# A two-layer decoder trunk on one core: first mixer's indexer and memory products in plain fp32, others in three products, new order of first loads

## Chip, cores and metric

The kernel runs on one core of one Trainium2 chip. The metric is the device time of one launch in microseconds, the median over several runs. Below, PE is TensorE (matmuls), PEld its weight loads, DVE VectorE, ACT ScalarE, POOL GpSimd, SP the SyncE queue that issues the loads.

## The reference, cut to what matters

512 tokens of width 1024 pass two layers. Each layer is `x += Mix(RMSNorm(x))`, then `x += SwiGLU(RMSNorm(x))`; a last RMSNorm follows. Layer 0 mixes by an indexer: eight small heads score every earlier key, the 128 best keys of a query are kept, and 12 heads (4 key/value heads, rotary) attend to those.

```python
logits = einsum('bqhd,bsd->bqhs', qib, ki)                  # 8 indexer heads, one shared key
score = einsum('bqhs,bqh->bqs', relu(logits), wib)
score = where(key_pos <= t_pos, score, NEG)
_, idx = top_k(score, min(256, seq // 4))                   # 128 keys
# 12 query heads attend to k[idx], v[idx]: softmax(q k / 8) v
# 4 memory heads, in both layers:
kv = rms_norm(mem, g_mem) @ w_mem_kv                        # 256 memory tokens
mo = softmax(qm @ kv_keys / 8) @ kv_values
x = x + concatenate([mix, mo]) @ w_out
```

Layer 1 mixes by dilated windows and attends to the same 256 memory tokens with its own weights. Everything is float32.

## The kernel before

Activations are kept transposed: `xT` holds eight tiles (k = 0 to 7) of 128 features x 512 tokens. A projection gives 128 output features x 512 tokens in one PSUM bank, over eight steps k. Each step is made of three matmuls in the type fp32r (`proj_steps`, `projs`, lines 217 to 227 with 213 to 215): weights and activations are split into a high part, rounded on ScalarE, and a low part, the rest, subtracted on VectorE or POOL (`_split2`, lines 48 and 51). High x high, high x low and low x high are summed. Value projections have tokens on the partitions and 256 columns (`token_major`). Attention scores take two heads at once, on rows 0 to 63 and 64 to 127 of the array, each again in three products (`scores`, line 414). Products of probabilities with values, transposes by the identity, the row that spreads the norm factors (`row`, line 268) and two of layer 1's value products (line 1017) are plain fp32.

TensorE executes in the order of the program; the other engines' order is planned by the compiler. Weights come in 1 MB loads of two chunks through two buffers (`wf`), split chunks lie in three buffers each for high and low (`wh`, `wl`). PSUM has banks by tag: acc 2, S 3, T 2, O 1.

`run` issues the first loads: gains, then x tiles and the first two weight chunks in turn, with frequencies and positions after the fourth x tile. `layer0` then runs so:

1. `angles` makes sine and cosine of the positions and writes them to DRAM, from where `angle_table` reads them back spread over the partitions. `prep` scales x by the norm's gains, splits it and sums its squares.
2. Five chunks of `in0` belong to the indexer: chunk 0 (the key and the head weights) and chunk 1 step by step together, then 2, 3 and 4. `ssq_cols` and `row` make the norm factors; `rope` rotates each result and splits it. `memory_load` and `memory_squares` (squares and sums both on POOL) start on the memory.
3. Chunk 5 (first key pair) starts; the column sums of the memory follow on TensorE (`ssq_cols(mem_parts)`, line 256), and then `logits` (relu on ScalarE, weighted sums on VectorE, lines 756 to 762), woven with chunk 5 and the value products of `value_steps`.
4. `memory_split`, the second key pair, two chunks of memory queries (`plain`), keys and values of the memory (`memory_kv`), then `memory_attention` woven with four query chunks. `topk` runs beside it on VectorE: 16 rounds of MAX8 and MATCH_REPLACE (lines 695, 696) for three blocks of queries, and a closing step (line 700).
5. 18 score units of the 12 heads, `exp_scores` (line 595) with the selection as bias, transposes and value products; between them the last two query chunks, layer 1's memory keys and values (`memory_ahead`, which loads the memory again, splits it and keeps the results in DRAM) and the output projection.

Then come `ffn(0)`, `layer1` and `ffn(1)`, all in three products but for what was named.

## Time and profile before

| | |
|---|---|
| median of 3 runs | 1267.03 us (1263.38 to 1268.05) |
| profiled execution | 1261.48 us, span 1259.8 us |
| mean granted clock of TensorE | 0.978 |
| busy, share of the span: PE / DVE / ACT / POOL | 95% / 46% / 40% / 31% |
| chain that ended last: PE / DVE / DMA | 78% / 13% / 3% |

The profile is of one execution. A busy time is the time in which at least one instruction of the engine ran; matmuls overlap, so a matmul's own duration is longer than its share, and the distance between starts is the better measure. The granted clock is given as a share of 2.4 GHz; its lower level is 1.2 GHz.

### The profile page before, as it was taken

To read this page: it belongs to the slowest core of one execution; us is meant where nothing else is said; L and a number is where in the kernel's file an instruction comes from. 1 tells how busy PE (TensorE), PEld (TensorE's weight loads), DVE (VectorE), ACT (ScalarE), POOL (GpSimd) and SP (SyncE) were. 2 spreads that over 40 slices of the span, in tenths; PEclk is the share of its full clock that TensorE was granted. 3 is DMA by queue.
4 is the path that set the end of the run, shared out by engine and by line. 5 is a ranking of instruction groups with operands and counts; after the bars stand their busy time and mean duration, and the time that the engine had idled before them with its cause. 6 is when DMAs were issued, how large, how long until landed. Compare 5 with 4: busy or idle time off the path is not lost.

```text
span 1259.8 us, 14831 instructions
## 1 busy us (share of the span) xinstructions
PE 1191.5 (95%) x5804; PEld 963.8 (77%) x5804; DVE 585.3 (46%) x1058; ACT 499.7 (40%) x865; POOL 385.7 (31%) x240
## 2 busy tenths in 40 slices
PE   6688989999999999999998999999999999999997
PEld 5467767677888888888887778887788888888886
DVE  7789986548433333322224544449533333332112
ACT  5564566524332233223223666545223223322222
POOL 4637374336122221121222223224222222211222
PEclk9789998999999999999999999999899999999999
DMA  5402222111222222222323120121122222222221
GB/s 180 137 34 70 82 90 99 56 49 68 100 101 88 84 97 100 100 62 104 110 105 127 67 71 34 68 67 67 67 100 101 94 81 93 101 92 92 92 92 67
DMA packets 30211, 109.96 MB, mean 87 GB/s; under 512 B 2494, under 2 KB 12094, under 8 KB 21694
## 3 DMA queue, kind: packets, MB, share of 16 engines
q1 hardware_dynamic: 29598, 108.50, 24.4%
q8 instruction: 45, 0.74, 0.2%
q10 hardware_dynamic: 544, 0.52, 0.1%
q14 instruction: 24, 0.20, 0.1%
HBM read 105.74 MB, written 3.28 MB: 87 GB/s over the span
## 4 chain that ended last, share of the span: by engine, by line
PE 78%; DVE 13%; DMA 3%; ACT 2%; POOL 2%; issue 2%; SPq 0%; DVEq 0%; POOLq 0%; ACTq 0%
PE psS L227 5%; PE psS L226 5%; PE psS L225 5%; PE psT L226 3%; PE psT L227 3%; PE psT L225 3%; PE psacc L227 3%; PE psacc L226 3%; PE psacc L225 3%; PE psacc L200 3%; PE psS L200 3%; PE psS L202 3%; PE psS L201 3%; PE psS L414 3%; PE psacc L202 3%; PE psacc L201 3%
## 5 line engine op out<-in xcount | busy, mean ns | idle before, releaser
L51 POOL TENSOR_TENSOR wl<-wf,wh 128x1024 fp32r<-128x1024 f32 x96 | 233.7, 2436 | 636.3 <-ACT wh L48 594.0
L48 ACT CAST wh<-wf 128x1024 fp32r<-128x1024 f32 x176 | 181.2, 1031 | 512.8 <-issue 164.2
L51 DVE TENSOR_TENSOR wl<-wf,wh 128x1024 fp32r<-128x1024 f32 (+1 forms) x93 | 116.0, 1247 | 90.9 <-ACT wh L48 90.9
L225 PE MATMUL psS<-xh,wh 128*128 128x512 f32 x296 | 117.8, 398 | 7.5 <-ACT wh L48 7.5
L227 PE MATMUL psS<-xh,wl 128*128 128x512 f32 x296 | 118.4, 400 | 2.6 <-DVE wl L51 2.6
L226 PE MATMUL psS<-xl,wh 128*128 128x512 f32 x296 | 117.6, 397 | 2.8 <-DVE xl L310 2.8
L227 PE MATMUL psT<-xh,wl 128*128 128x512 f32 x200 | 80.1, 400 | 0.0
L226 PE MATMUL psT<-xl,wh 128*128 128x512 f32 x200 | 79.8, 399 | 0.0
L225 PE MATMUL psT<-xh,wh 128*128 128x512 f32 x200 | 79.5, 398 | 0.0
L227 PE MATMUL psacc<-xh,wl 128*128 128x512 f32 x192 | 76.6, 399 | 0.0
L226 PE MATMUL psacc<-xl,wh 128*128 128x512 f32 x192 | 76.2, 397 | 0.0
L225 PE MATMUL psacc<-xh,wh 128*128 128x512 f32 x192 | 75.9, 395 | 0.0
L225 PEld LDWEIGHTS psS<-xh,wh 128*128 128x128 f32 x296 | 56.6, 191 | 20.3 <-ACT wh L48 7.5
L226 PEld LDWEIGHTS psS<-xl,wh 128*128 128x128 f32 x296 | 56.6, 191 | 16.8 <-DVE xl L310 3.3
L227 PEld LDWEIGHTS psS<-xh,wl 128*128 128x128 f32 x296 | 56.5, 191 | 15.4 <-DVE wl L51 4.0
L294 POOL TENSOR_TENSOR ssq<-ssq,t 128x512 f32<-128x512 f32 (+1 forms) x34 | 50.9, 1496 | 54.9 <-ACT t L284 53.8
L213 PE MATMUL psacc<-xh,wh 128*128 128x512 f32 x144 | 62.7, 435 | 0.0
L652 DVE TENSOR_TENSOR raw<-psacc,R 128x512 f32<-128x512 f32 x22 | 15.2, 691 | 100.8 <-PE psacc L227 100.8
L215 PE MATMUL psacc<-xh,wl 128*128 128x512 f32 x144 | 58.0, 403 | 0.0
L214 PE MATMUL psacc<-xl,wh 128*128 128x512 f32 x144 | 57.8, 401 | 0.0
L627 DVE TENSOR_TENSOR xT<-xT,psacc 128x512 f32<-128x512 f32 x44 | 30.0, 684 | 38.8 <-PE psacc L202 38.6
L339 POOL TENSOR_TENSOR raw<-raw,table 128x512 f32<-128x512 f32 x21 | 27.9, 1329 | 58.4 <-ACT raw L336 39.8
(339 smaller groups left out, 2729.0 us busy)
## 6 DMA issues: line engine op xcount, KB each, us to landing
wf<-in_gu SPq DMA_DIRECT2D x44, 1024.0 KB
wf<-in_dn SPq DMA_DIRECT2D x16, 1024.0 KB
wf<-in_in SPq DMA_DIRECT2D x13, 1024.0 KB
wf<-in_dn SPq DMA_DIRECT2D x16, 384.0 KB
wf<-in_v SPq DMA_DIRECT2D x3, 1024.0 KB
xT<-in_x SPq DMA_DIRECT2D x8, 256.0 KB
wf<-in_mk SPq DMA_DIRECT2D x2, 1024.0 KB
wf<-in_mv SPq DMA_DIRECT2D x2, 1024.0 KB
```

The lines of the kernel that those rows point to most:

```text
L48: nc.scalar.copy(hi, src)
L51: lo_engine.tensor_tensor(out=lo, in0=src, in1=hi.bitcast(F32), op=ALU.subtract)
L200: mm(out, wh[k], xh[k], start=first and k == 0, stop=False)
L201: mm(out, wh[k], xl[k], start=False, stop=False)
L202: mm(out, wl[k], xh[k], start=False, stop=last and k == n - 1)
L213: mm(out, wh[:, s], xh[k], start=k == 0, stop=False)
L214: mm(out, wh[:, s], xl[k], start=False, stop=False)
L215: mm(out, wl[:, s], xh[k], start=False, stop=k == KT - 1)
L225: mm(out, wh[:, s], xh[k], start=k == 0, stop=False)
L226: mm(out, wh[:, s], xl[k], start=False, stop=False)
L227: mm(out, wl[:, s], xh[k], start=False, stop=k == KT - 1)
L294: engine.tensor_tensor(out=parts[part], in0=parts[part], in1=sq, op=ALU.add)
```

## The change

- Order of the first loads: chunk 0, then all of x, chunk 1, frequencies, positions. TensorE first issues 14 matmuls of 128 columns whose result isn't used; `angles` moves behind the first two products and the column sums.
- `scaled` scales x on VectorE and keeps it whole; ScalarE squares, VectorE sums. The five indexer chunks are plain fp32 on it (`fp32_steps`), from the loaded buffer. `halves` splits x only after them, for the remaining chunks, which stay in three products with the low parts of chunk 5 from VectorE and of chunks 6 to 14 from POOL.
- Rotated queries and keys of the indexer and of the 12 heads stay whole (no split after `rope`); logits and scores of the first mixer are one fp32 product each. All of `rope_steps` multiplies and adds on POOL. Relu of the logits is done in place in PSUM, and their banks alternate between the tags S and acc.
- The memory, for both layers, is scaled on ScalarE and multiplied in fp32 from the loaded buffers; its squares move to ScalarE, the sums stay on POOL and are used after six of the twelve logit units. The memory is not loaded a second time. Keys kept for layer 1 are whole and half as large, and layer 1's memory queries and scores are fp32 as well.

```diff
+    def plain_chunks(self, name, order):
+        src = self.io[name]
+        for a in range(0, len(order), 2):
+            m = min(2, len(order) - a)
+            w = self.load(src[order[a]:order[a] + m].rearrange("t p n -> p t n"), [m, KT * 128])
+            for j in range(m):
+                yield w[:, j]
+    def fp32_steps(self, out, w, x):
+        for k in range(KT):
+            self.nc.tensor.matmul(out, w[:, k * 128:(k + 1) * 128], x[k], start=k == 0, stop=k == KT - 1)
+            if k % 2:
+                yield 1
+    def fp32_tokens(self, out, w, ks, x, b):
+        n = out.shape[-1]
+        for k in ks:
+            self.nc.tensor.matmul(out, x[k][:, b], w[:, k * n:(k + 1) * n], start=k == 0, stop=k == KT - 1)
...
+    def scaled(self, gi):
+        nc = self.nc
+        xg = []
+        add, parts = self.squares()
+        for k in range(KT):
+            if k % 4 == 0:
+                big = self.big("xg", F32)
+            t = big[:, (k % 4) * S:(k % 4 + 1) * S]
+            nc.vector.tensor_scalar(t, self.xT[:, k], self.gains[:, gi, k:k + 1], None, op0=ALU.mult)
+            add(self.xT[:, k], 0, nc.vector)
+            xg.append(t)
+        return xg, parts
+    def halves(self, x):
+        xh, xl = [], []
+        for k in range(KT):
+            if k % 4 == 0:
+                bh, bl = self.big("xh"), self.big("xl")
+            b = slice((k % 4) * S, (k % 4 + 1) * S)
+            _split2(self.nc, bh[:, b], bl[:, b], x[k], self.nc.vector)
+            xh.append(bh[:, b])
+            xl.append(bl[:, b])
+        return xh, xl
...
         (mul or nc.gpsimd).tensor_tensor(out=sw, in0=sw, in1=sn, op=ALU.mult)
-        (add or nc.vector).tensor_tensor(out=raw, in0=raw, in1=sw, op=ALU.add)
+        last = hi if lo is None and twice is None else raw
+        (add or nc.vector).tensor_tensor(out=last, in0=raw, in1=sw, op=ALU.add)
         if twice is not None:
-            nc.vector.tensor_tensor(out=raw, in0=raw, in1=twice, op=ALU.mult)
+            nc.vector.tensor_tensor(out=hi, in0=raw, in1=twice, op=ALU.mult)
+        if lo is None:
+            return hi
...
+        if units[0][2] is None:
+            for out, q, _, k, _, rows, qs, ks in units:
+                mm(out, q[rows, qs], k[rows, ks], start=True, stop=True)
+            return
...
-            add(m, 0, self.nc.gpsimd, self.nc.gpsimd)
+            add(m, 0, self.nc.gpsimd)
...
+    def memory_scaled(self, l, mem):
+        g = self.big("mg", F32)
         for k in range(KT):
...
+            self.nc.scalar.activation(g[:, k * MEM:(k + 1) * MEM], mem[k], AF.Copy,
+                                      scale=self.gains[:, 1 if l == 0 else 4, k:k + 1])
+        return [g[:, k * MEM:(k + 1) * MEM] for k in range(KT)]
+    def memory_kv(self, l, x):
+        for w in self.plain_chunks(f"mk{l}", [0, 1]):
             p = self.psum("acc")
+            for n, _ in enumerate(self.fp32_steps(p[:, :MEM], w, x)):
...
+            yield self.plain(p, self.mem_row, 1.0, "km", n=MEM)
+        w = self.load(self.io[f"mv{l}"], [KT * 256])
         for i in range(2):
...
+            self.fp32_tokens(p, w, range(4), x, b)
             yield None
+            self.fp32_tokens(p, w, range(4, KT), x, b)
...
     def layer0(self):
         nc, mm = self.nc, self.nc.tensor.matmul
-        self.angles()
-        xh, xl, parts = self.prep(0, early=4, squares=(1, 3))
-        first = [self.wsplit(self.first[j], nc.vector) for j in range(2)]
-        pk, pq = self.psum("S"), self.psum("S")
-        self.projs([(pk, first[0]), (pq, first[1])], xh, xl)
-        ws = itertools.chain(self.chunks("in0", [2, 3]), self.chunks("in0", [4, 5]),
-                             self.chunks("in0", list(range(6, 15)), lo=("gpsimd", "gpsimd")))
+        idle = self.psum("T")
+        for _ in range(14):
+            mm(idle[:, :128], self.ones, self.ones, start=True, stop=True)
+        x, parts = self.scaled(0)
+        ws = itertools.chain(self.first, self.plain_chunks("in0", [2, 3, 4]))
...
+        pk, pq = product("S"), product("S")
         cols = self.ssq_cols(parts)
+        self.angles()
...
-                ps = [self.psum("S") for _ in range(2)]
+                tag = ("S", "acc")[(j + i) % 2]
+                ps = [self.psum(tag) for _ in range(2)]
...
-                    t = self.tmp(("t", "o")[s])
+                    t = ps[s]
...
-            dst.append(self.rope(p, cs, sn, *out, add=nc.gpsimd, split=nc.gpsimd, mul=mul))
+            dst.append(self.rope(p, cs, sn, out, None, add=nc.gpsimd, mul=nc.gpsimd))
...
         index_q(3, p3)
-        steps = itertools.chain(rope_steps(K, kb[:, 0], kb[:, 1], tag="O"), value_steps())
-        next(steps)
+        xh, xl = self.halves(x)
+        ws = itertools.chain(self.chunks("in0", [5], lo=("vector",)), self.chunks("in0", list(range(6, 15)), lo=("gpsimd", "gpsimd")))
+        steps = itertools.chain(rope_steps(K, kb[:, 0], tag="O"), value_steps())
+        mem_parts = self.memory_squares(mem)
+        every = itertools.chain.from_iterable(logits(j) for j in range(4))
+        for _ in itertools.islice(steps, 4):
+            pass
+        _weave(itertools.islice(steps, 3), itertools.islice(every, 6), nb=2)
         self.mem_cols = self.ssq_cols(mem_parts, n=2, keep=True)
-        every = itertools.chain.from_iterable(logits(j) for j in range(4))
-        _weave(itertools.islice(steps, 12), every, nb=1)
+        _weave(itertools.islice(steps, 3), every, nb=2)
...
-        fill = itertools.chain(queries(2), self.memory_ahead())
+        fill = itertools.chain(queries(2), self.memory_ahead(mem))
...
+        nc.sync.dma_start(self.first[0], self.io["in0"][0])
         for k in range(KT):
             nc.sync.dma_start(self.xT[:, k], self.io["x"][k * 128:(k + 1) * 128, :])
-            if k < 2:
-                nc.sync.dma_start(self.first[k], self.io["in0"][k])
-            if k == 3:
-                nc.sync.dma_start(self.freq, self.io["freq"])
...
+        nc.sync.dma_start(self.first[1], self.io["in0"][1])
+        nc.sync.dma_start(self.freq, self.io["freq"])
```

## Rows read from the trace of the kernel before

**Rows 1.** Table by stretch: from:to, length, busy time (instructions) by engine, PEclk, DMA share.

```profile
0.00:100.00 100.00, 72.99 (x344) 56.08 (x345) 78.86 (x116) 57.86 (x102) 51.45 (x40) 0.90 0.36 121
100.00:170.00 70.00, 63.20 (x350) 50.04 (x348) 69.50 (x179) 37.84 (x78) 41.64 (x29) 0.95 0.19 68
170.00:290.00 120.00, 111.12 (x678) 82.46 (x677) 69.65 (x179) 61.29 (x162) 53.24 (x37) 0.97 0.21 69
...
320.00:677.00 357.00, 357.00 (x1561) 292.81 (x1560) 113.06 (x142) 105.36 (x129) 79.97 (x36) 1.00 0.26 95
```

**Rows 2.** TensorE's waits, 0 to 300 us: sum, times, longest.

```profile
PE psacc L256 <- POOL ssq L294: 9.1, 1, 9.1
PE psS L414 <- DVE nx L595: 8.2, 7, 3.7
...
PE psS L414 <- ACT t L756: 5.5, 3, 3.9
```

**Rows 3.** The chain that ended last, 25 to 105 us: start, duration, what.

```profile
31.96 11.39 DMA mem<-in_mem
...
59.45 1.03 PE psacc L256 x4
```

**Rows 4.** Order of time, VectorE, in the selection: start, duration, what.

```profile
104.66 1.47 DVE L695 MAX8 m<-score 128x8 f32<-128x512 f32 x3
...
107.63 1.47 DVE L695 MAX8 m<-score 128x8 f32<-128x512 f32 x3
...
168.84 4.22 DVE L700 TENSOR_SCALAR score<-score 128x512 f32<-128x512 f32 x3
```

**Rows 5.** Order of time, TensorE: memory scores, then the first mixer's scores.

```profile
131.33 0.39 PE L414 MATMUL psS<-km,qmh 64*128 64x256 f32 x2
...
172.16 0.33 PE L414 MATMUL psS<-k,qh 64*128 64x128 f32 x2
...
182.00 0.50 PE L414 MATMUL psS<-k,qh 64*128 64x512 f32 x2
...
182.90 0.50 PE L213 MATMUL psacc<-xh,wh 128*128 128x512 f32 x1
```

**Rows 6.** Table by stretch, TensorE alone: length, busy (matmuls), PEclk, DMA.

```profile
26.58:32.10 5.52, 5.52 (x26) 1.00 0.23 66
113.82:119.40 5.58, 5.58 (x49) 1.00 0.54 188
7.46:18.65 11.19, 8.58 (x18) 1.00 0.90 333
```

**Rows 7.** Order of time, TensorE: plain fp32 products of 512 and 256 columns.

```profile
319.43 1.02 PE L268 MATMUL psacc<-raw,ones 128*128 128x512 f32 x2
...
320.52 0.39 PE L226 MATMUL psS<-xl,wh 128*128 128x512 f32 x1
...
773.06 2.13 PE L1017 MATMUL psacc<-wf,xT 128*128 128x256 f32 x8
```

**Rows 8.** DMA in 0 to 60 us, 40 slices of 1.5 us.

```profile
GB/s 0 109 249 352 373 392 360 396 408 284 374 262 0 0 0 0 0 0 44 86 80 89 145 258 225 215 244 312 199 47 55 27 8 213 415 63 49 102 56 52
```

**Rows 9.** Order of time, VectorE: first use of the sine table, and layer 1's memory split.

```profile
42.93 0.69 DVE L339 TENSOR_TENSOR raw<-raw,table 128x512 f32<-128x512 f32 x1 [4.02 <-DMA table<-saved]
...
188.67 2.06 DVE L486 SCALAR_TENSOR_TENSOR ml<-wf,gains,mh 128x256 fp32r<-128x256 f32 x5
```

**Rows 10.** Order of time, SP and ScalarE: a weight load's issue and its first use.

```profile
113.92 0.34 SPq L176 DMA_DIRECT2D wf<-in_mv  x1
...
118.76 1.99 ACT L48 CAST wh<-wf 128x1024 fp32r<-128x1024 f32 x2 [1.84 <-DMA wf<-in_mv]
```

**Rows 11.** VectorE's groups, 101.6 to 172 us: line, operation, shapes, busy, mean ns.

```profile
L51 DVE TENSOR_TENSOR wl<-wf,wh 128x1024 fp32r<-128x1024 f32 x2 | 4.5, 2262 | 0.0
...
L51 DVE TENSOR_TENSOR km<-t,km 128x256 fp32r<-128x256 f32 x2 | 1.9, 975 | 0.0
```

More of the change, by code (lines that the diff above doesn't have):

```diff
@@ L490, in memory_kv @@
-    def memory_kv(self, l, m):
-        mh, ml = m
-        xh = [mh[:, k * MEM:(k + 1) * MEM] for k in range(KT)]
-        xl = [ml[:, k * MEM:(k + 1) * MEM] for k in range(KT)]
-        for w in self.chunks(f"mk{l}", [0, 1]):
+            self.nc.scalar.activation(g[:, k * MEM:(k + 1) * MEM], mem[k], AF.Copy,
[3 more added lines that the diff above has]
+        for w in self.plain_chunks(f"mk{l}", [0, 1]):
@@ L514, in memory_ahead @@
+            t = self.slot("vm", F32)[:, :256]
+            self.values(p, self.mem_cols[:, i:i + 1], t)
+            yield t
+    def memory_ahead(self, mem):
         nc = self.nc
-        mem = self.load(self.io["mem"].rearrange("(k p) n -> p k n", p=128), [KT, MEM])
-        m = self.memory_split(1, [mem[:, k] for k in range(KT)])
-        self.kept = self.dram.tile([4, 128, 512], F32, name="kept")
+        x = self.memory_scaled(1, mem)
+        self.kept = self.dram.tile([4, 128, 256], F32, name="kept")
@@ L518, in memory_ahead @@
         n = 0
-        for r in self.memory_kv(1, m):
-            if r:
-                n_cols = 512 if n < 2 else 256
-                nc.sync.dma_start(self.kept[n][:, :n_cols], r[1].bitcast(F32)[:, :n_cols])
+        for r in self.memory_kv(1, x):
+            if r is not None:
+                nc.sync.dma_start(self.kept[n], r)
                 n += 1
@@ L526, in memory_back @@
     def memory_back(self):
-        ts = []
-        for n in range(4):
-            ts.append(self.slot("kept", F32R if n < 2 else F32))
-            n_cols = 512 if n < 2 else 256
-            self.nc.sync.dma_start(ts[n].bitcast(F32)[:, :n_cols], self.kept[n][:, :n_cols])
-        self.mem_kv = [(t[:, :MEM], t[:, MEM:]) for t in ts[:2]], ts[2:]
+        ts = [self.slot("kept", F32)[:, :256] for _ in range(4)]
+        for n, t in enumerate(ts):
+            self.nc.sync.dma_start(t, self.kept[n])
+        self.mem_kv = ts[:2], ts[2:]
     def memory_attention(self, qm, early):
@@ L764, in logits, with rope_steps @@
                 yield 1
-        kb = self.big("k").rearrange("p (c n) -> p c n", c=4)
+        kv = self.big("kv", F32)
+        kb = kv[:, :1024].rearrange("p (c n) -> p c n", c=2)
+        V = kv[:, 1024:].rearrange("p (i n) -> p i n", i=NT)
         K, Q, qm = [], [], []
-        def index_steps(j):
-            p = self.psum("T")
-            yield from self.proj_steps(p, next(ws), xh, xl)
-            index_q(j, p)
-        def rope_steps(dst, *out, tag="acc", mul=None):
+        def rope_steps(dst, out, tag="acc"):
             p = self.psum(tag)
             yield from self.proj_steps(p, next(ws), xh, xl)
-            dst.append(self.rope(p, cs, sn, *out, add=nc.gpsimd, split=nc.gpsimd, mul=mul))
-        V = self.big("v", F32).rearrange("p (i n) -> p i n", i=8)
+            dst.append(self.rope(p, cs, sn, out, None, add=nc.gpsimd, mul=nc.gpsimd))
         def value_steps():
@@ L808, in layer0 @@
             qm.append(self.plain(p, R, 0.125, "qm", engine=nc.gpsimd))
-        mem = [r[0] for r in self.memory_kv(0, mem) if r]
-        self.mem_kv = mem[:2], mem[2:]
+        kept = [r for r in self.memory_kv(0, xm) if r is not None]
+        self.mem_kv = kept[:2], kept[2:]
         self.masks()
@@ L816, in queries @@
             for c in range(n):
-                yield from rope_steps(Q, self.slot("qh"), self.slot("ql"))
+                yield from rope_steps(Q, self.slot("q", F32))
         _weave(queries(4), mema, nb=1, na=1)
```

78 lines of the change are left out of this document (21 added, 57 removed).

## Prediction

> **What bounds the kernel now.** I read the stretch table first [rows 1]. From 320 to 677 us (the first FFN) TensorE is busy for all of 357 us, and the change doesn't touch that stage or the second FFN. So whatever moves must move in the first mixer, which ends some 20 us before that stretch, and in layer 1's memory attention. In 0 to 100 us TensorE is busy for 73 us, at a mean granted clock of 0.90, so a part ran at the lower level of 1.2 GHz. In 100 to 170 us VectorE is busy for 69.5 of 70: this is the top-k selection. From 170 to 290 us TensorE is the fuller engine, 111 of 120.
>
> Then the waits of TensorE up to 300 us [rows 2]. The longest, 9.1 us, is for POOL's sums of squares of the memory. The chain of waits puts its end at 59.45 us; the load it hangs on was in at 31.96 + 11.39 = 43.35 us, and POOL's squares and sums filled the 16 us between [rows 3]. TensorE executes in program order, so the logits, which need nothing of the memory, stand behind it. 5.5 us of waits are the logits' own (PSUM banks held until ScalarE has read them), 8.2 us those for the biased scores after the selection.
>
> The selection needs the last logits. One round of 16 takes 107.63 - 104.66 = 2.97 us, 47.5 us in all [rows 4]. Its first round starts one such step ahead of the row shown, at 101.7 us, and the closing step at 168.84, 67 us later: 19.6 us of other VectorE work are woven in. The first scores of the mixer proper issue at 172.16 us [rows 5]. So the path is: index products, memory stall, logits, selection, scores; behind that it is TensorE.
>
> **The price of fp32.** A chunk in three products, 8 steps of 3 matmuls with 512 columns, took 5.5 us, 0.69 a step; two chunks with 256 columns took 5.58 us, 0.35 a step [rows 6]. One fp32 product shows as two records. For 512 columns: the product that spreads R starts at 319.43, and the second matmul after it at 320.52; less the 0.23 us of the one between, that is 0.86 us. For 256 columns: eight records in 2.13 us, the last lasting some 0.40, give 0.247 each, 0.49 a product [rows 7]. The Trainium skill ("FP8 and Floating Point Precision", TensorE Precision Notes) says that true FP32 makes four passes through the array, which speaks against the change; by it a step would cost 4/3 of 0.69, an estimate of 0.92 us, and the five index chunks 1.6 us more than in the sum below. The row gives 0.86, so the sum goes by rows: 0.88 a step, with 0.86 and 0.98 (two 256-column products of 0.49) as bounds.
>
> **Part by part, up to the scores.**
> Loads and start. The first weight chunk is issued first, then the eight tiles of x, then chunk 1, frequencies, positions. The DMA slices of 1.5 us [rows 8] add up to 0.54 MB at 4.5 us, 2.2 at 9 and 2.75 at 10.5. So chunk 0 and x (2.6 MB) are in at about 10 us, chunk 1 at 11.5. No split stands before a product any more, only one scaling on VectorE. Before, the first 18 matmuls took 11.2 us, 8.6 of them busy [rows 6], with waits between them and at the lower clock. The 14 idle products run from 1 to about 6.5 us, so the clock should be up when x is there. From 6.2 us: five chunks x 8 steps x 0.88 = 35.2, plus 1 us for the column sums and 0.9 for R: the last index product ends near 43.3 us.
> Angles. Their issue moves behind all of x, so positions land with the last loads, at about 12 us. VectorE's queue ahead of them is shorter by two weight splits. Then the round trip through DRAM, for which VectorE waited until 42.93 us [rows 9]. I take it 4 us earlier. The ropes need about 10 us of VectorE and run beside the last index products and the key chunk.
> The splits of x become extra passes, eight each on ScalarE and VectorE. A VectorE operation of 512 columns takes 0.69 us [rows 9], so 5.5 us, which lie between 24 and 40 us, where VectorE waits for the tables. Without that cover they come on the path.
> Key chunk: 5.5 us, to 49. Then the value weights: their buffer is free only when the last fp32 product is done (43.3). A 1 MB load took 118.76 - 113.92 = 4.84 us from issue to use [rows 10], cast and low part 2.2: 50.4 us, a stall of 1.5.
> Logits. Six half value products of 1.4 us, twelve logit units, the column sums of the memory. A unit of 512 columns took 182.90 - 182.00 = 0.90 us with the changes of tile form [rows 5]; in fp32, with the two heads of a pair overlapping in the array as now, 0.86 and about 0.1 for the change of form. So nothing is added: 12 x 0.71 = 8.5 us for the three widths. The sum is 50.4 + 8.4 + 8.5 + 1 = 68 us. Five banks in place of three hold the logits. The memory sums now come after six units, with the squares on ScalarE: POOL keeps half of its 16 us, from about 41 us on, so I put the 9.1 us wait at zero. VectorE's 24 accumulations, at no more than 0.7 us each, run beside it. With 3 us of latency behind the last unit and 4 us of small stalls the selection starts at about 75 us, not 101.7.
> Selection. 47.5 us, 4 us of closing steps, and of the 19.6 us woven in 11 stay: two weight splits (4.5) and the low parts of the memory keys (1.9) are gone [rows 11], and three rope multiplies of 0.69 go to POOL. So VectorE is done at about 138 us.
> TensorE in that time: two half value products 2.8, second key chunk 5.5, two memory-query chunks 11, memory keys and values 32 products x 0.49 = 15.7 (were 11.2), a row 0.5, and the four query chunks with the memory attention woven in, 131.33 to 172.16 before [rows 5], 40.8 us; of these I take off 2 for waits on VectorE. 74.3 us from 70 us on: 145. TensorE has become the later of the two. Against 172.2: **27 us earlier**.
> POOL gains rope multiplies and loses low parts, one for one, and at 41.6 of 70 us [rows 1] it is no bound.
>
> **After the scores.** Of the 8.2 us of waits for biased scores [rows 2] most stood behind layer 1's memory split on VectorE (five of its operations from 188.67 us [rows 9]). With the split gone I take 6 us back, and 2.5 us of low clock after it. Layer 1's keys and values cost 32 x (0.49 - 0.35) = 4.5 us more. The scores come out even, as above. Net **-4 us**. In layer 1 the kept memory is smaller and two query splits go; the memory scores cost the same: 0 to -2, taken as 0.
>
> Sum: 27 + 4 = 31 us. The profiled execution has 1261.5 us (span 1259.8, 1.7 around it), 5.5 under the median of the three runs. 1261.5 - 31 = 1230.5; on the scale of the median **1236 us**.
>
> **Bounds.** No row shows fp32 products on 64 rows, so their overlap is bounded from both sides: as full as in the three-product form, or none. In columns per pair of heads the logits have 4608, the scores 7680, the memory scores 2 x 2048: 16,384, or 32 times 512 at 0.86 = 27.5 us more if pairs run one after the other. I take the overlap; the nearest row is the same code in the same tile form. On the other side: no stalls at all (-7), all of the 8.2 us back (-2), 0.86 a step (-1), layer 1 (-2): 12 us better.
>
> **Rivals.**
> Pairs in sequence (0.10). The 27.5 us come onto TensorE, which is the bound from 145 us on. The gain shrinks to 3 or 4 us: 1263. Against it: six matmuls of 512 columns on 64 rows fit into 0.90 us now, which only overlap allows. The Trainium skill ("TensorEngine Tiling (Array Packing)", Key Properties) says that different tiles load and multiply in parallel. By that rule this rival wouldn't occur; no row here shows it for fp32.
> The start isn't shortened (0.15). The index ropes, not the products, set the first logits: if the DRAM round trip of the tables still ends at 42.9 us, VectorE takes the x splits (5.5 us) ahead of the ropes and POOL's sums come late, the logits gain only half of the 27 us. Then 13 + 4: 1250.
> Held weight buffers (0.10), the slow side. An fp32 product reads the loaded buffer itself and frees it at its last step; there are two buffers. The split form frees it some 3 us after landing, far ahead. Eight hand-overs change that way (two index loads, the value weights, two query loads, two of layer 1's memory, the first output chunk). Each one exposed costs 4.84 us of load, and 3.5 of cast and POOL split where the next user is split: 8.3 us. I counted 1.5 us for the one I found exposed. From four exposed (33 us) the gain is gone; with five, 41 against 31, it is slower: 1277.
> The forecast as summed has 0.65.
>
> **How the numbers follow.** The forecast's own range is 1224 to 1248 (12 better; 12 worse if half the start's gain is lost in stalls). To leave out no more than 2 in 10 the range takes in the start rival and the pairs in sequence: 1222 to 1263. A measurement of this kernel can tell about 0.5%, 6.3 us. Faster: forecast 0.65, start 0.15 and a little of the pairs: 0.82. Same: the rest of the pairs and a share of the buffers: 0.10. Slower: 0.08.
>
> **What would show it.** Right: the first MAX8 near 75 us, the first scores near 145, the FFN's first products some 30 us earlier; no TensorE wait above 3 us for the memory's sums; fp32 records of 0.43 us at 512 columns; VectorE nearly full in the selection. The pairs are in sequence if the logit records of both heads lie end to end. The start is wrong if the first logit issues later than 57 us. Buffers are exposed if TensorE waits above 3 us for wf or wh more than twice. The prediction is wrong altogether if the first scores issue after 165 us.

## The result, and the profile after

The changed kernel takes **1257.28 us** (median of 20 runs, 1247.48 to 1262.89) beside 1263.5 us for the kernel before (20 runs, 1260.28 to 1273.14): a ratio of 0.993, 95% interval 0.991 to 0.995. Forecast were 1236 us with a range of 1222 to 1263: the direction and the range held, the size did not, 31 us forecast and 6 measured. (The 1236 stands on the scale of three early runs, median 1267.03; against the twenty it would be some 3.5 us less.) The profiled execution took 1258.64 us (span 1256.9).

The table by stretch, as in [rows 1] (busy time of PE, PEld, DVE, ACT, POOL, then PEclk and DMA):

```profile
0.00:100.00 100.00, 86.81 (x321) 53.71 (x322) 60.48 (x137) 53.63 (x103) 28.10 (x29) 0.90 0.35 117
100.00:170.00 70.00, 64.61 (x310) 48.42 (x309) 53.38 (x155) 35.69 (x77) 36.02 (x25) 1.00 0.25 88
170.00:290.00 120.00, 115.18 (x604) 79.61 (x603) 56.84 (x156) 57.37 (x158) 41.97 (x29) 1.00 0.17 58
...
320.00:677.00 357.00, 357.00 (x1546) 290.57 (x1545) 109.28 (x139) 102.07 (x125) 79.96 (x36) 1.00 0.26 95
```

VectorE has far less to do up to 290 us (171 us busy for 218 before), and little came of it: TensorE is busy for 87 of the first 100 us and not 73, and still stops. Its waits up to 100 us, as in [rows 2]:

```profile
PE psO L235 <- ACT wh L48: 5.9, 1, 5.9
PE psacc L452 <- DVE score L785: 2.4, 2, 1.6
PE psO L237 <- DVE wl L51: 2.3, 1, 2.3
```

The 9.1 us on the memory's sums are gone; in their place TensorE waits for the split of the key chunk's weights (`wh` is the rounded high part, `wl` the low part; `xh` and `xl` are those of x). Why, the order of time shows. The lines are cut from the views of ScalarE, VectorE, TensorE and SP:

```profile
19.08 1.17 ACT L372 COPY raw<-psS 64x512 f32<-64x512 f32 x2
...
34.32 0.69 DVE L382 TENSOR_TENSOR raw<-raw,table 128x512 f32<-128x512 f32 x1 [4.38 <-DMA table<-saved]
...
34.96 0.42 ACT L306 ACTIVATE ssq<-mem 128x256 f32<-128x256 f32 x1 [12.36 <-DMA mem<-in_mem]
...
38.31 7.13 PE L207 MATMUL psT<-xg,wf 128*128 128x512 f32 x16 [1.12 <-DMA wf<-in_in]
...
42.17 2.16 ACT L48 CAST xh<-xg 128x512 fp32r<-128x512 f32 x4
...
43.60 3.62 DVE L51 TENSOR_TENSOR xl<-xg,xh 128x512 fp32r<-128x512 f32 x5
...
50.22 1.05 ACT L48 CAST wh<-wf 128x1024 fp32r<-128x1024 f32 x1
...
51.32 0.79 PE L235 MATMUL psO<-xh,wh 128*128 128x512 f32 x1 [5.87 <-ACT wh L48]
...
54.83 0.33 SPq L176 DMA_DIRECT2D wf<-in_vw  x1
```

ScalarE stands for 12.4 us in front of the memory's first square, with everything behind it in its queue: rope copies, the rounding of x, the rounding of the chunk, which begins only at 50.2. So the key chunk begins at 51.3, not at the 43.3 at which I had the last index product end. Two of these 8 us are the index products' own, which ended at 45.4 (38.31 + 7.13); 5.9 are the wait.

**Three profiles of the same kernel.** Two more were taken beside the experiments ("again", "third"). Starts in us:

| | before | after | again | third | forecast |
|---|---|---|---|---|---|
| first key product | 48.9 | 51.3 | 51.3 | 51.1 | 43 |
| first logit | 63.2 | 64.2 | 63.4 | 63.6 | 52 |
| first MAX8 | 101.7 | 93.5 | 87.7 | 92.8 | 75 |
| first score unit | 172.2 | 166.8 | 161.0 | 166.1 | 145 |
| row sum of the first FFN | 319.4 | 312.9 | 307.3 | 312.0 | 288 |
| first FFN, from there to layer 1's sums | 357.9 | 362.6 | 357.9 | 357.9 | 357.9 |
| span | 1259.8 | 1256.9 | 1247.8 | 1250.3 | 1229 |

In the column of the forecast, 52 is the 50.4 at which the value weights were to be split and half a value product of 1.4; 288 and 1229 are the times before, less 31.

Up to the first logit the three agree within 1 us. Two things then differ from execution to execution. One is the granted clock in the logits (TensorE alone: length, busy, PEclk, DMA); first the page's execution, then "again":

```profile
70.00:80.00 10.00, 8.19 (x32) 0.71 0.01 2
80.00:90.00 10.00, 10.00 (x53) 0.77 0.00 0
```

```profile
70.00:80.00 10.00, 8.16 (x51) 1.00 0.01 2
80.00:90.00 10.00, 9.98 (x61) 1.00 0.00 0
```

The busy share is the same, the clock is not. A mean of 0.71 and then 0.77 over 10 us each makes some 10 us at 1.2 GHz, half of the full clock, in the one; the other has 2.4 GHz throughout. "Third" (0.67 and 0.82) is like the first. The first MAX8, VectorE's first step of the selection, comes 5.8 us apart, again the page's execution first:

```profile
93.53 1.48 DVE L721 MAX8 m<-score 128x8 f32<-128x512 f32 x3 [0.40 <-POOL score L789]
```

```profile
87.71 1.48 DVE L721 MAX8 m<-score 128x8 f32<-128x512 f32 x3 [0.40 <-POOL score L789]
```

The other thing is the FFN's duration (last section).

### The profile page after: what moved, and what is told of

It is laid out like the page before. It is cut to its first block, busy times and chain, and to the rows that moved or that the text cites. A ratio compares the mean times of both kernels' runs of the same rounds, so it can differ in the third digit from the quotient of the medians.

```text
span 1256.9 us, 14343 instructions
## 1 busy us (share of the span) xinstructions
PE 1209.4 (96%) x5624; PEld 952.3 (76%) x5624; DVE 530.6 (42%) x1024; ACT 484.8 (39%) x852; POOL 345.6 (27%) x218
## 4 chain that ended last, share of the span: by engine, by line
PE 78%; DVE 10%; DMA 4%; ACT 3%; issue 3%; POOL 1%; SPq 0%; DVEq 0%; ACTq 0%; POOLq 0%
PE psS L248 5%; PE psS L247 5%; PE psS L249 5%; PE psT L247 3%; PE psT L248 3%; PE psT L249 3%; PE psacc L247 3%; PE psacc L248 3%; PE psacc L249 3%; PE psacc L222 3%; PE psS L222 3%; PE psS L224 3%; PE psS L223 3%; PE psacc L224 3%; PE psacc L223 3%
## 5 line engine op out<-in xcount | busy, mean ns | idle before, releaser
L51 POOL TENSOR_TENSOR wl<-wf,wh 128x1024 fp32r<-128x1024 f32 x90 | 216.9, 2411 | 643.6 <-ACT wh L48 590.5
L48 ACT CAST wh<-wf 128x1024 fp32r<-128x1024 f32 (+1 forms) x163 | 167.6, 1029 | 516.5 <-issue 166.1
L51 DVE TENSOR_TENSOR wl<-wf,wh 128x1024 fp32r<-128x1024 f32 x86 | 104.0, 1210 | 88.6 <-ACT wh L48 88.6
L248 PE MATMUL psS<-xl,wh 128*128 128x512 f32 x272 | 107.7, 396 | 2.8 <-DVE xl L332 2.8
L247 PE MATMUL psS<-xh,wh 128*128 128x512 f32 x272 | 108.2, 398 | 0.0
L249 PE MATMUL psS<-xh,wl 128*128 128x512 f32 x272 | 106.9, 393 | 0.0
L248 PE MATMUL psT<-xl,wh 128*128 128x512 f32 x184 | 73.3, 398 | 0.0
L249 PE MATMUL psT<-xh,wl 128*128 128x512 f32 x184 | 72.8, 396 | 0.0
L316 POOL TENSOR_TENSOR ssq<-ssq,t 128x512 f32<-128x512 f32 (+1 forms) x31 | 42.4, 1367 | 96.2 <-ACT t L306 61.0
L248 PEld LDWEIGHTS psS<-xl,wh 128*128 128x128 f32 x272 | 51.3, 188 | 14.8 <-DVE xl L332 3.3
L379 ACT COPY raw<-psacc 32x512 f32<-32x512 f32 x72 | 41.6, 578 | 6.1 <-DVE raw L376 5.1
```

The costliest lines, as they stand in the source:

```text
L48: nc.scalar.copy(hi, src)
L51: lo_engine.tensor_tensor(out=lo, in0=src, in1=hi.bitcast(F32), op=ALU.subtract)
L247: mm(out, wh[:, s], xh[k], start=k == 0, stop=False)
L248: mm(out, wh[:, s], xl[k], start=False, stop=False)
L249: mm(out, wl[:, s], xh[k], start=False, stop=k == KT - 1)
L316: engine.tensor_tensor(out=parts[part], in0=parts[part], in1=sq, op=ALU.add)
```

## The experiments

I held three theories, one after the other. By each the start is late because something stands late in the queues of ScalarE and VectorE: S says the splits of x, W the splits of the key chunk's weights, O whatever was planned ahead of the instruction that TensorE waits for. The rivals have letters, too. By Q the start hangs on something other than x. By P and T the time won at the start is lost again before the scores, by V the value weights come late in their turn, by C the clock and the logits' own pace hold the start.

Results, in us; the ratio is to the kernel before on the same chip. Each edited kernel has one profile. The first two columns of starts are good to about 1 us, as the three profiles above show; from the last logit on the same kernel differs by 5 to 6 us, and a smaller difference there can be the execution's:

| kernel | first key product | first, last logit | first MAX8 | first score | row sum | ratio (95%) |
|---|---|---|---|---|---|---|
| after, again | 51.3 | 63.4, 84.1 | 87.7 | 161.0 | 307.3 | 0.991 (0.988 to 0.994) |
| after, third | 51.1 | 63.6, 89.2 | 92.8 | 166.1 | 312.0 | 0.994 (0.991 to 0.996) |
| u3 | 56.0 | 70.4, 91.5 | 95.5 | 170.5 | 317.9 | 0.999 (0.997 to 1.002) |
| e1 | 52.0 | 64.3, 90.0 | 93.6 | 166.9 | 313.2 | 0.992 (0.990 to 0.995) |
| e2 | 52.4 | 65.1, 85.7 | 89.3 | 162.6 | 312.7 | 0.994 (0.991 to 0.996) |
| e4 | 51.7 | 64.5, 83.4 | 86.9 | 160.2 | 309.9 | 0.993 (0.991 to 0.995) |
| e5 | 52.2 | 63.7, 82.1 | 85.7 | 160.6 | 306.8 | 0.990 (0.988 to 0.992) |
| e6 | 44.1 | 59.2, 85.3 | 88.8 | 162.1 | 308.5 | 0.993 (0.990 to 0.995) |
| e8 | 46.0 | 62.8, 84.3 | 88.3 | 161.5 | 307.4 | 0.992 (0.988 to 0.995) |
| e9 | 43.5 | 56.5, 82.6 | 86.1 | 159.4 | 305.9 | 0.988 (0.985 to 0.991) |
| e10 | 43.9 | 59.1, 87.2 | 90.7 | 165.7 | 315.2 | 0.993 (0.990 to 0.995) |
| e11 | 49.3 | 59.8, 84.1 | 87.7 | 162.6 | 312.0 | 0.988 (0.985 to 0.991) |
| e12 | 45.3 | 64.8, 84.8 | 88.4 | 163.3 | 309.5 | 0.989 (0.986 to 0.991) |
| e13 | 44.3 | 57.5, 79.8 | 83.2 | 158.2 | 304.5 | 0.992 (0.990 to 0.994) |
| e14 | 56.4 | 63.8, 82.1 | 86.1 | 161.1 | 308.3 | 0.993 (0.991 to 0.995) |

**e1, x split early** (the line stood behind the last index rope):

```diff
         self.angles()
+        xh, xl = self.halves(x)
```

> The changed kernel with one move: the rounding and the low parts of x (halves) are emitted right behind the angles, ahead of the index tables, queries and ropes, so that they stand before the ropes and the memory's squares on ScalarE and VectorE. Theory S (the start): in the changed kernel the key chunk waited 5.9 us for its rounded weights, 2.3 us for their low part, and some 3 us went to the low clock behind these waits, because the splits of x stood behind the ropes. Then the first key product comes by 47 us (51.3 in the changed kernel), the first logit by 55 to 57 (64.2), the first MAX8 near 84 (93.5), and the time is 7 to 10 us under the changed kernel, a ratio to the kernel before of 0.985 to 0.988. Rival P (the time is taken up again before the first scores by the selection or by TensorE): the first logit comes as early, but the first score unit stays within 2 us of 166.8, and so does the time (ratio 0.992 to 0.994). Rival Q (the index weights' low parts or the memory, not x, set the chunk): the first key product stays within 1.5 us of 51.3.

Rival Q came. The first key product still waits, for longer; ScalarE begins to round its weights only at 50.9:

```profile
52.00 0.80 PE L235 MATMUL psO<-xh,wh 128*128 128x512 f32 x1 [7.60 <-ACT wh L48]
```

**e2, no idle matmuls** (the loop of 14 taken out).

> The changed kernel without the 14 idle matmuls ahead of the first products. If they hold the clock up at the start as the trace shows (granted clock 1.00 from 0 to 40 us), the index products run at 1.2 GHz for some of the time and the first MAX8 comes 2 to 4 us later, the time 2 to 4 us above the changed kernel. Rival: the arrival of x bounds the start, the products catch up while waiting for it, and first MAX8 and time move by 1 us at most.

At the first MAX8 (89.3) nothing shows beyond the spread of one kernel, which is the rival. TensorE waits 6.6 us for VectorE's scaled x and begins its first product there, where the changed kernel begins it at 6.8. The products don't quite catch up: the column sums behind the first two of them start at 23.2 for 21.2, the key chunk 1 us later.

**e4, the memory's scaling on POOL**; **e5, e1 and e4 together.**

```diff
-            self.nc.scalar.activation(g[:, k * MEM:(k + 1) * MEM], mem[k], AF.Copy,
-                                      scale=self.gains[:, 1, k:k + 1])
+            self.nc.gpsimd.tensor_scalar(g[:, k * MEM:(k + 1) * MEM], mem[k], self.gains[:, 1, k:k + 1],
+                                         None, op0=ALU.mult)
```

> The changed kernel with layer 0's scaling of the memory by its gains (8 groups of 128 by 256) on POOL in place of ScalarE, where it stood ahead of the relus of the logits (waits of TensorE on the scores of 0.8, 1.6 and 0.2 us there). If ScalarE's queue sets the pace of the logits (27 us for the 18 forecast), the logits take 2.5 to 4 us less, the first MAX8 comes 2 to 4 us earlier, and the time is 2 to 4 us under the changed kernel. Rival (VectorE's weighting of the relus sets it): the logits take as long within 1 us, and the time moves by 1 us at most, or rises as POOL and VectorE share the memory.

> The early splits of x and the memory's scaling on POOL together. Theory S with the logits bound by ScalarE: the first MAX8 near 81 us, the first score unit near 155, the time 10 to 13 us under the changed kernel, a ratio to the kernel before of 0.982 to 0.985. If the two overlap (the scaling is out of the way already when the logits begin, or begins to bind because they begin earlier), less than the larger of the two alone plus 1 us.

From the first to the last logit it is 19.0 and 18.5 us, against 20.7 in "again" at the same full clock from 70 us on: the scaling ahead of the relus cost 2 us. The medians (1254.96 and 1250.17) are 2 and 7 us under the changed kernel's first measure (1257.28), and 2 above and 2 under its second (1252.63). For e5 that is not the 10 to 13 expected, since e1 in it gave nothing; for e4 it is no verdict on the time.

**e6, the key chunk's weights in a buffer of their own** (on top of e5); **e8, that edit alone.**

```diff
         mem = self.memory_load()
+        w5 = self.big("w5", F32)[:, :1024]
+        nc.sync.dma_start(w5, self.io["in0"][5])
+        w5 = self.wsplit(w5, nc.vector)
...
+        ws = itertools.chain([w5], self.chunks("in0", list(range(6, 15)), lo=("gpsimd", "gpsimd")))
```

> The early splits of x, the memory's scaling on POOL, and the key chunk's weights loaded into a buffer of their own right behind the memory's load call, so that they are rounded and split before the ropes and the memory's squares. The early splits of x alone left the key chunk at 52.0 us (51.3 in the changed kernel), since ScalarE rounded the weights only at 50.9, behind the squares and the ropes. Theory W (the key chunk's weights, loaded into the second buffer that an fp32 product holds to its last step and then rounded behind ScalarE's other work, set the start): the key chunk begins within 1 us of the end of the last index product (44 to 46 us), the first logit comes at 51 to 55, the first MAX8 at 72 to 77, the first score unit at 145 to 152 and the FFN's row sum at 291 to 299 (306.8 with the two edits before it), the time is 8 to 14 us under theirs (1250): 1236 to 1242, a ratio to the kernel before of 0.978 to 0.985. Rival T (TensorE's work from there to the scores, or the selection on VectorE, takes it up again): the first MAX8 comes as early, the FFN's row sum at 303 us or later. Rival V (the value weights are late in their turn): a wait of TensorE for wf or wh of 3 us or more behind the key chunk, and the logits not before 58.

> The changed kernel with that one edit, the key chunk's weights in a buffer of their own; x is split where it was and ScalarE scales the memory. Theory W: the low parts of x (43.6 to 51.5 us in the changed kernel) are now the last to come, the key chunk begins at 45 to 49, in step with them, and the first logit at 54 to 58; the time is 3 to 8 us under the changed kernel. If x and the weights bind alike, the key chunk stays within 1.5 us of 51.3 and the time within 2 us.

Theory W is right on the key chunk (44.1 and 46.0) and wrong on what follows; in the end rival V came. TensorE's waits up to 100 us in e6:

```profile
PE psacc L452 <- DVE score L793: 4.0, 1, 4.0
...
PE psT L441 <- ACT wh L48: 3.4, 1, 3.4
...
PE psT L443 <- DVE wl L51: 2.5, 1, 2.5
```

It now waits for the value weights and then for the first weighted logits: 7 us won at the key chunk, none seen at the first MAX8.

**u3, the first loads in the old order.**

> The changed kernel with the first loads in the order of the kernel before (x and the two first weights by turns, the positions after the fourth part of x). The index products then begin with the second load of x and not earlier, the sine tables come 3 to 5 us earlier as the positions do. Theory W or S: the key chunk waits for splits on ScalarE and VectorE all the same, so that the time moves by 2 us at most. Rival: the order of the first loads carries the gain of the start, and the time rises by 3 to 6 us.

Its rival won: 1263.54 us, beside 1252.63 for the changed kernel on the same chip, so the whole measured gain is gone. The loads themselves are a small part. The index products begin at 7.2 for 6.8 us, and the column sums behind the first two at 23.0 for 21.2. In the plan of this kernel the memory's first square also stands ahead of the first rope copies, which the changed kernel has at 19.1:

```profile
36.50 0.42 ACT L306 ACTIVATE ssq<-mem 128x256 f32<-128x256 f32 x1 [16.61 <-DMA mem<-in_mem]
36.93 1.17 ACT L372 COPY raw<-psS 64x512 f32<-64x512 f32 x2
```

But this place in the queue can't be the whole cause. e2's plan has it as well, and e2 kept its gain (1254.84):

```profile
34.74 0.42 ACT L306 ACTIVATE ssq<-mem 128x256 f32<-128x256 f32 x1 [16.29 <-DMA mem<-in_mem]
...
36.74 1.17 ACT L372 COPY raw<-psS 64x512 f32<-64x512 f32 x2
```

What else u3 loses by is open. Its waits for the key chunk are longer (6.3 and 4.8 us; 4.6 and 3.4 in e2), and its granted clock is 0.83 from 40 to 50 us (1.00 in e2).

**e9, the last index rope on VectorE and ahead of the tables** (on top of e6); **e10, with it the memory's squares on POOL**; **e11, e10 with x split where it was**; **e12, the squares on POOL alone.**

```diff
-            self.rope(p, ci, si, qi[:, b], None, mul=(nc.vector, nc.vector, nc.vector, nc.gpsimd)[j])
+            self.rope(p, ci, si, qi[:, b], None, mul=nc.vector)
...
+        index_q(3, p3)
         cs, sn = self.tables(R, 0)
-        index_q(3, p3)
```

The squares (e10 to e12):

```diff
-            add(m, 0, self.nc.gpsimd)
+            add(m, 0, self.nc.gpsimd, self.nc.gpsimd)
```

> The kernel with the own buffer, early splits and the memory's scaling on POOL, and in it the last index rope on VectorE (POOL did it) and ahead of the rope tables of the mixer. In the run before, TensorE did the key chunk at 44.06, but the first logits only at 59.2 (it waited 3.4 and 2.5 us for the value weights' split, which stood behind the memory's squares on ScalarE), and the first weighted logit only at 67.7: VectorE stood 7.8 us on the last rope, which POOL did behind the tables that came from memory late, and ScalarE's first relu stood behind the rounding of a chunk that landed at 61.4. Theory O (queue order: each engine works in the order that was planned, and the start costs what the latest planned-ahead instruction costs): the 4.0 us wait on the first score goes, the first MAX8 comes 3 to 6 us earlier (83 to 86), the first score unit 73 us behind it as in all runs so far (156 to 159), the time 3 to 6 us less. Rival (VectorE's extra 2 us and the relus behind the landing cost as much): first MAX8 within 1.5 us of 88.8.

> The kernel with the last index rope on VectorE, and the memory's 8 squares on POOL too, so that ScalarE rounds the value weights as soon as they have landed. Theory O: the value weights are rounded at 46 to 49 us and not at 52.4, the first logit comes at 50 to 54, the first MAX8 at 74 to 79, the first score unit at 147 to 152, the row sum of the FFN at 294 to 299, the time 1240 to 1245 with the FFNs at their quicker pace. Rival (POOL becomes the late one: 16 operations of 0.8 us from 42 us on, and the low part of the value weights and the tables behind them): a wait of TensorE for wl of 3 us or more, and the first MAX8 no earlier than 83.

> The same kernel with the splits of x back behind the ropes, where ScalarE now has no squares ahead of them. The sine tables and ropes then come some 5 us earlier than with the early splits (ropes from 30 and not from 36 us), the splits of x fill VectorE after them. Theory O: the key chunk begins at 44 to 47, the first logit at 50 to 54, the first MAX8 within 2 us of the kernel with the early splits. If VectorE's low parts of x (8 of 0.7 us, more beside POOL) bind, the first logit comes 3 us or more later than there.

> The changed kernel with that one edit, the memory's squares on POOL and not on ScalarE. ScalarE stood idle 12.4 us for the memory's landing with the roundings of x queued behind it. Theory O: the roundings of x and of the key chunk move up, the key chunk begins at 46 to 49 us (51.3 in both profiles of the changed kernel), the first logit at 58 to 61 (63.4, 64.2), the first MAX8 at 82 to 85 (87.7 at full clock), the time 3 to 5 us under the changed kernel. If the ropes behind it hold it all the same, within 1 us of 51.3 and of the time.

e9 gained 2.7 us at the first MAX8 (3 to 6 expected). e10, e11 and e12 missed: the first logit comes at 59.1 and 59.8 for 50 to 54, and at 64.8 for 58 to 61. Each has a reason of its own.

In e10 its own rival came. TensorE waits 3.7 us for the value weights' low part (1.7 in e9). VectorE begins that part at 55.4 (52.8 in e9), behind instructions that wait for POOL, which is now longer at the memory:

```profile
PE psT L443 <- DVE wl L51: 3.7, 1, 3.7
```

```profile
53.07 0.17 DVE L114 MEMSET t<- 128x128 f32 x1 [0.68 <-POOL ssq L316]
...
54.52 0.81 DVE L121 CAST window<-o 128x256 bf16<-128x256 f32 x1 [0.43 <-POOL o L118]
...
55.38 1.21 DVE L51 TENSOR_TENSOR wl<-wf,wh 128x1024 fp32r<-128x1024 f32 x1
```

POOL's work also slows VectorE's step of a rope: 0.69 us with POOL idle, 1.1 to 1.3 beside it in e10:

```profile
43.62 1.10 DVE L382 TENSOR_TENSOR raw<-raw,table 128x512 f32<-128x512 f32 x1
...
45.78 1.23 DVE L382 TENSOR_TENSOR raw<-raw,table 128x512 f32<-128x512 f32 x1
```

But e9, with the sums alone on POOL, has 1.21 and 1.23 for these two steps; of this kind only the next one parts e10 from it (1.29 for 0.69).

In e11 the last index chunk waits 2.5 us for its weights and then takes 10.1 us for 7.1, at a granted clock of 0.71 from 40 to 50 us, so the key chunk begins at 49.3:

```profile
39.80 10.11 PE L207 MATMUL psT<-xg,wf 128*128 128x512 f32 x16 [2.52 <-DMA wf<-in_in]
```

e8 waits as long there (2.45 us) and its clock stays at 1.00.

e12 is the plainest test of the queue. With the squares off ScalarE, and no other edit, the chunk's weights are rounded at 43.3 for 50.2 and the key chunk begins at 45.3. It stops two matmuls later, for 9.6 us, on the low part of its weights, which now stands behind VectorE's work:

```profile
43.33 1.04 ACT L48 CAST wh<-wf 128x1024 fp32r<-128x1024 f32 x1
...
45.31 0.79 PE L235 MATMUL psO<-xh,wh 128*128 128x512 f32 x1
...
55.90 0.79 PE L237 MATMUL psO<-xh,wl 128*128 128x512 f32 x1 [9.57 <-DVE wl L51]
```

The low ratios of e9, e11 and e12 are against a median of 1266.11 us for the kernel before, 3 to 4 us above those of the other chips; their own medians are 1251 to 1252.

**e13, e9 with the key chunk's rope behind the logits; e14, with it the low parts of x on POOL; the changed kernel beside them.**

```diff
-            dst.append(self.rope(p, cs, sn, out, None, add=nc.gpsimd, mul=nc.gpsimd))
+            late.append(p)
...
+        K.append(self.rope(held[0], cs, sn, kb[:, 0], None, add=nc.gpsimd, mul=nc.gpsimd))
...
-            _split2(self.nc, bh[:, b], bl[:, b], x[k], self.nc.vector)
+            _split2(self.nc, bh[:, b], bl[:, b], x[k], self.nc.gpsimd)
```

> The kernel with the own buffer, early splits, scaling on POOL and the last index rope on VectorE, and in it the key chunk's rope behind the logits. In the run before, the first relu stood at 64.66 on ScalarE behind the key rope's copies (61.69 to 64.64), the rounding of chunk 6 (60.61) and the last index rope's copies (58.25); TensorE waited 4.4 us for it and its clock was 0.67 from 60 to 70. Theory O (queue order): the first relu comes at 61 to 62, the wait falls to 1 to 2 us, the first MAX8 comes 3 to 5 us earlier (81 to 83), the first score unit 73 us behind it (154 to 157), the time 3 to 5 us under that run's 1251. Rival C (the clock and the logits' own pace hold it: 24 to 26 us from the first to the last logit in three of the runs): the first MAX8 within 1.5 us of 86.

> The same, and the low parts of x (8 of 128 by 512) on POOL, which is idle up to 40 us, in place of VectorE. VectorE then finishes the angles some 5 us earlier (sine tables back at 35 and not at 41 us), and with them the index ropes, the value weights' rounding (50.7) and the last index rope (61.4). Theory O: the first logit at 50 to 53, the first MAX8 at 76 to 80, the first score unit at 149 to 153, the time 1242 to 1247 with the FFNs at their quicker pace. Rival: POOL's work slows VectorE's scaling and sums of x by sharing the memory port from 8 to 25 us, the sine tables come no earlier than 39, and the first MAX8 stays within 1.5 us of the kernel beside it.

> The changed kernel unaltered, on the same chip as the two above and with a third profile. Expected: the key chunk at 51.3 again and the waits of 5.9 and 2.3 us ahead of it, the first MAX8 at 87.7 (clock 1.00 from 70 to 84 us) or 93.5 (clock 0.71 to 0.77 there), each FFN at one of its two durations.

> The changed kernel again, unaltered, for a second profile beside the edited ones: which of the differences between two profiles are those of two executions. If the low clock from 50 to 60 us and from 70 to 84 follows from the waits in front of it, both come again, and the first MAX8 within 1 us of 93.5; if it is a matter of the execution, the clock there and the logits (25.8 us from first to last) differ by some us. The first FFN took 362.6 us in one profile and 357.9 in the kernel before with the same instructions: expected is one of the two again.

e13 went the way of theory O, by less than expected: the first relu at 62.8 (64.7 in e9; 61 to 62 expected), the wait 2.4 us (4.4; 1 to 2), the first MAX8 at 83.2 (2.9 us earlier; 3 to 5), the row sum 15 us ahead of the kernel before. Its clock was 1.00 from 60 to 70 us, 0.67 in e9, and one profile of each can't tell whether the edit or the execution did that. Its median, 1250.53, is 2.8 us under that of the changed kernel on the same chip (1253.31); the intervals overlap.

e14 shows both sides of POOL. VectorE's groups in 6 to 30 us, e14 and then e13:

```profile
L316 DVE TENSOR_TENSOR ssq<-ssq,t 128x512 f32<-128x512 f32 x7 | 6.8, 966 | 0.3 <-ACT t L306 0.2
L348 DVE TENSOR_SCALAR xg<-xT,gains 128x512 f32<-128x512 f32 x8 | 6.7, 864 | 5.3 <-DMA xT<-in_x 5.3
```

```profile
L316 DVE TENSOR_TENSOR ssq<-ssq,t 128x512 f32<-128x512 f32 x7 | 4.8, 687 | 0.2 <-ACT t L306 0.2
L348 DVE TENSOR_SCALAR xg<-xT,gains 128x512 f32<-128x512 f32 x8 | 3.8, 483 | 5.6 <-DMA xT<-in_x 5.6
```

Beside POOL both operations take 1.4 to 1.8 times as long, the ropes start late (the sine table is first used at 43.6 us, 41.3 in e13), the last index chunk waits 7.4 us for its weights and the key chunk begins at 56.4. But then nothing stands ahead of the relus, the clock is 1.00, and the logits take 18.3 us: the 18 of the forecast without its small stalls. So the pace of the logits was sized rightly; they were not let run at it.

## Why the prediction was right and wrong, step by step

**Right: the price of fp32.** Eight steps of 512 columns take 7.03 us, 0.88 a step, as forecast from [rows 7]:

```profile
29.83 7.03 PE L207 MATMUL psT<-xg,wf 128*128 128x512 f32 x16
...
64.16 0.70 PE L452 MATMUL psacc<-ki,qi 64*128 64x256 f32 x4
64.69 0.81 PE L452 MATMUL psS<-ki,qi 64*128 64x384 f32 x4
```

Each product stands as two records. The last two lines are pairs of heads: 256 columns for both heads in 0.53 us from start to start, where two products of 0.44 one after the other would take 0.88. The rival "pairs in sequence" is out. This agrees with the rule of the Trainium skill ("TensorEngine Tiling (Array Packing)", Key Properties) that tiles multiply in parallel, here for fp32.

**Right: TensorE bounds from the logits to the scores.** From the first MAX8 to the first score unit it is 73.3 us in all three profiles of the changed kernel (70 by the forecast's 75 and 145), and 73 to 75 in the edited ones. The memory's 32 fp32 products take 13.9 us in it, 0.43 each, for the 15.7 forecast. In "again" VectorE is busy all through the selection, as forecast, but ends it at 143 us and has the masks done 18 us before the first scores.

**Wrong: the start.** The sum ran the index products to 43.3 us, the key chunk right behind them to 49, and the logits from 50.4 to 68. That is TensorE's work; of the splits that the key chunk needs, two terms failed:

- *The key chunk's own weights* were put at nothing: "Key chunk: 5.5 us, to 49" has no term for their rounding and low part. It was these that TensorE waited for, 5.9 and 2.3 us.
- *The splits of x* were to "lie between 24 and 40 us, where VectorE waits for the tables". VectorE did wait, up to 34.3. But a low part needs the rounding on ScalarE first, and that stood behind the memory's first square: the roundings ran from 42.2, the low parts from 43.6 to 51.5. An idle engine is no cover for an instruction that stands behind the one it waits for.

The runs part the two. With x split early (e1) the key chunk begins at 52.0, no sooner. With its weights rounded early (e8), or with the squares taken out of ScalarE's queue (e12), it begins at 46.0 and 45.3. In both of these TensorE then waits for a low part (7.4 us for the value weights', 9.6 for the chunk's own), and the first logit gains next to nothing.

In time this is nearest to the rival "the start isn't shortened" (0.15), though not in its cause: the sine table was back early (34.3 for 42.9 us), and the queue order was late. The key chunk comes 8 us late, 6 of them by its wait. The first logit comes 12 late, since the chunk then stops 2.3 us for its low part and runs at a granted clock of 0.52 from 50 to 60 us; at 64 it is behind the 57 that the prediction named as a sign. By its strongest sign, first scores after 165 us, it is "wrong altogether" in two of three profiles (166.8 and 166.1; 161.0).

**Wrong: the clock in the logits.** 18 us were forecast, and 4 of small stalls; 25.8, 20.7 and 25.6 were measured. 20.7 is within that, and 2 us of it are the scaling ahead of the relus (e4). The other 5 us go with the clock, which was low between 70 and 90 us in two of three executions and had no term in the sum. Why it falls in one execution and not in another, with waits of 2.6, 2.3 and 2.4 us for VectorE in the logits, is open.

**Half right: the value weights.** I had them load from 43.3, in the buffer of the index products. They went out at 54.8, at the end of the key chunk's low part. No wait came of it, since the chunk was late as well; e6 shows the wait (3.4 and 2.5 us) once it is not. Of the rival "held weight buffers" little more was seen in the changed kernel: one load was exposed, for 1.1 us.

**Half right: after the scores.** I forecast -4 us; from the first score unit to the row sum 147.3 became 146.1, 146.3 and 146.0. The 8.2 us for the biased scores (`nx`, [rows 2]) fell to 2.8 (6 back forecast, 5.4 found) and the clock stayed at 1.00 from 190 to 200 (0.68 before). Against it stand layer 1's dearer keys and values (4.5 us forecast, some 2.7 by the 0.43 us a product above, an estimate) and waits for the transposed probabilities and a row of factors (`pt`, `frow`) of 2.4 us for 0.6. How these add up to little more than 1 us isn't shown.

**The sum.** At the first MAX8 27 us were forecast and 8 to 14 came. The best edited kernel reached 18.5, and where an edit took one wait away TensorE met the next. The waits of e6, e12 and e13 show that TensorE is held there by what stands in the queues of ScalarE and VectorE, not by its own work. That 75 us can be reached is not shown: where an edited kernel and the changed one ran on the same chip, no edited median lies clear below. Why the planner put the squares and ropes ahead was not tried, nor was an earlier load of the memory, which is issued from 23.5 us on and ends ScalarE's wait at 35.0.

That 1257 lies in the range of 1222 to 1263 is luck. The forecast's own range ended at 1248 and the start rival at 1250; the rest was there for the pairs in sequence, which didn't occur.

## What to carry over

Cost a change at the start of a kernel queue by queue, not engine by engine: write down what stands ahead of each instruction that the critical engine will wait for, and when that lands. An idle stretch covers only what is next in that queue; here one square that waited for a load held the roundings for which TensorE then stood 5.9 us. Taking one such instruction out isn't enough when the next queue has its own. And take a second profile before explaining 5 us: the same kernel gave a first MAX8 at 93.5 and at 87.7.

## What the runs showed of the hardware

**Two durations of one FFN.** With the same instructions and no wait, the first FFN took 357.9 us in 15 of the 17 profiles and 362.6 in 2; the second, from its row sum to the end, 364.1 to 364.4 in 12 and 368.7 to 369.2 in 5. TensorE alone, first the page's execution (362.6), then "again" (357.9):

```profile
400.00:420.00 20.00, 20.00 (x88) 1.00 0.28 106
420.00:440.00 20.00, 20.00 (x87) 1.00 0.29 106
...
560.00:580.00 20.00, 20.00 (x89) 1.00 0.23 78
```

```profile
400.00:420.00 20.00, 20.00 (x89) 1.00 0.28 101
420.00:440.00 20.00, 20.00 (x89) 1.00 0.23 65
...
560.00:580.00 20.00, 20.00 (x89) 1.00 0.21 73
```

By the starts of the matmuls they follow one another every 0.2333 us for some 240 us, and every 0.2289 otherwise, at a granted clock of 1.00 both times: 2% of pace that the clock row doesn't show. Its cause is open. Between the page's execution and "again" it makes 4.6 us, and the clock in the logits 5.8; the spans differ by 9.1. The 20 runs of the changed kernel spread over 15 us, two and a half times the gain that was measured; whether the same two things make that spread isn't shown.

**The clock after like waits.** After waits of 2.45 and 2.52 us for a load, the last index chunk took 7.1 us in e8 and 10.1 in e11, at granted clocks of 1.00 and 0.71 from 40 to 50 us.

**VectorE beside POOL.** Two-input operations of 512 columns went from 0.69 to between 1.1 and 1.3 us (e10), the one-input scaling from 0.48 to 0.86 (e14).
